# The second branch's projection as seven products of half blocks

## The chip, the cores and the metric

One core of one Trainium2 chip runs the program. The metric is the device time of one execution in microseconds. A core has TensorE (matmuls, results in PSUM banks), VectorE (DVE), ScalarE (ACT) and GpSimd (POOL), each with a queue of its own that is worked off in order, and SyncE (SP), which here only issues transfers. POOL issues transfers too, among them all that add to what lies at their destination.

## The reference, cut to what matters

One layer over 1024 prompt tokens and 32 sample tokens, 1056 columns in all; the model width is 1024.

```python
y_A = sink_attention(...)                 # (t, 1024)
y_B = rms_norm(hgrn2(...)) * silu(og_B)   # (t, 1024)
mix = sigmoid(gate_A) * (y_A @ W_brA) + sigmoid(gate_B) * (y_B @ W_brB)
x = x + rms_norm(mix @ W_out)
[a | u] = rms_norm(x) @ W_up;  a = conv3(a)
x = x + rms_norm((gelu(a) * u) @ W_down)
x = x + (pe @ W_ple) * sigmoid(x @ W_ple_gate)    # pe: (t, 256), the per-layer inputs
```

All inputs and outputs are float32.

## The kernel before

Every product of float32 matrices is made of three matmuls of rounded parts: a matrix is split into a rounded part (a cast on ScalarE, "hi") and a remainder (a subtraction on VectorE, "lo"), and hi x hi, hi x lo and lo x hi are added in PSUM. Activations lie with the features on the 128 partitions (8 tiles, k = 0 to 7) and tokens in the columns; the 1056 tokens are 4 groups of 264 (H), or 2 halves (p) of 2 groups (h).

The stages follow each other on TensorE: the head stage (input projections, attention, the recurrence with its heads 0 to 7; functions `group_out`, `tile_out` and the list `pieces`, beside which `small` and `at` put other work at counted places), branch A's projection, branch B's projection, the out projection, the per-layer input's product (`ple_product`), the up stage (22 units), the down stage, the gate. What is late in one stage moves all that follow.

Branch A's projection is made of seven products of half blocks instead of eight (`a_unit`, operands numbered i = 0 to 6): the weights are taken in 2 x 2 blocks of 512 x 512, the activations in 2 x 2 blocks (features halves a, token groups h), and sums of blocks stand for some of them. The sums lie in DRAM (`wa_d` of the weights, `sa_d` of the activations) and are made beside the head stage by accumulating POOL transfers (`block_sum`). `OPS` gives two phases: for each of 4 columns c first the products 0, 1, 2, then for each column 3, 4, 5, 6. One product for one column and both token halves is a step: 24 matmuls (k 4 x 3 parts x 2 halves). The steps are counted by `n_s`: 0 to 11 half steps, then to 33 whole ones. `beside(n)`, called at the end of a step, runs what `during(step, ...)` put there: loading an operand into a page of memory (`a_page`, `a_load`) and splitting it (`a_split`, `halves`). Pages are named places ("l0", "r6", ...), reused when the last reader is done. The weights of a step come through a ring of 8 buffers "wb": `a_raw` loads two at a time, `a_prepare` casts and subtracts.

After a step its results are read from PSUM: product 0 by ScalarE ("as"), the others by VectorE, which combines them ("R", "ac") and multiplies by the gate (1 + tanh, "ta"). Products 2 and 4 are written to `mx_d` in DRAM, products 5 and 6 stay in memory (`M_`).

Branch B's projection is plain: 8 columns x 4 groups, each 8 k x 3 matmuls (`block`, `product`), then gate, addition of branch A's part, and the split for the out projection (`Ra`, `Rb`) at lines 1758 and 1759 and `split`. Between the columns `p_cols` turns the per-layer inputs: 24 transposes of 88 columns, split, and written to `pc_d`, read again by `p_load`.

The out projection takes two halves p; for each p 8 columns c and the two groups. Beside its second half run the norm of the first (`pair_norm`: sums at line 1822, a chain of small VectorE instructions, rows at line 306), `x1_part` and `build_ops`, which make the up stage's operands. The up stage's first weights (`early_parts`, tiles "rw" and "pw") are split beside its first half. After it come the sums of the remaining norms, in a bank of the pool `tr` (two banks).

The order of the instructions within each engine is set by the framework's scheduler, which goes by its own model of durations and by the constraints `behind(...)` (not before the last instruction of an engine).

Of the kernel before, what the change touches and what calls it, by code (L numbers as in the profile page):

```python
# [59 lines left out]
def layer_kernel(  # L60
# [50 lines left out]
    ghh = cp.tile([P, 1], F32, name="ghh")  # L111
# [7 lines left out]
    mx_d = dp.tile([P, 2, 4, 2, H], F32, name="mx_d")  # L119
    wa_d = {o: dp.tile([P, 4, 512], F32, name=f"wa_d{o}") for o in (1, 3, 4, 6)}  # L120
    sa_d = {o: dp.tile([P, 4, 2, H], F32, name=f"sa_d{o}") for o in (1, 3, 4, 5)}
# [7 lines left out]
    pc_d = [dp.tile([P, 2, 2, H], F32, name=f"pc_d{g}") for g in range(4)]  # L129
# [36 lines left out]
    plan += [rows_cols(w_br_b, 0, c * P, P, KT) for c in range(8)]  # L166
# [150 lines left out]
    with right("ap") as ap:  # L317
# [287 lines left out]
        with tc.tile_pool(name="np", bufs=1, side="right", reuse_waits="tile") as np_:  # L605
# [85 lines left out]
            def derived():  # L691
# [8 lines left out]
                V.tensor_scalar(ghh[:], gvec[:, 48:49], 0.5, None, op0=ALU.mult)  # L700
# [386 lines left out]
    with right("bp") as bp:  # L1087
# [297 lines left out]
        def group_out(h, g):  # L1385
# [73 lines left out]
        sums = [lambda n=n, c=c: w_sum(n, c) for n in range(8) for c in range(2)]  # L1459
        for n, (dst, (o, src, acc)) in enumerate([(sa_d, y) for y in y_sums] + [(wa_d, a) for a in a_sums]):  # L1460
            sums.insert(2 * n, lambda d=dst[o][:], src=src, acc=acc: block_sum(d, src, acc))
        for n, f in enumerate(sums):
            at(26 + 11 * n // 2, f)
# [33 lines left out]
    A_ORDER = [(c, i) for ph in OPS for c in range(4) for i in ph]  # L1497
# [3 lines left out]
    at_h, at_l = ("r3", "r4", "l7", "l6"), ("l2", "l3", "l4", "l5")  # L1501
    at_y = (("r6", "r5"), ("r1", "r7"), ("r0", "r2"), ("l0", "l1"))

    def a_raw():

        k = len(raw_a)
        t = wp.tile([P, KT, P], F32, tag="wr", name=nm("wa"), bufs=2)
        raw_a.append(t)
        for a in range(2):
            c, i = A_ORDER[2 * k + a]  # L1510
            src = wa_d[i] if i in wa_d else av[:, i // 2 % 2 + i // 5, i // 5]
            dma(t[:, 4 * a:4 * a + 4], src[:, :, c * P:(c + 1) * P])

    def a_prepare(n):

        while len(ready_a) < min(n + 1, len(A_ORDER)):
# [5 lines left out]
            S.copy(t[:, 0], src)  # L1522
            V.tensor_tensor(t[:, 1], src, t[:, 0].bitcast(F32), op=ALU.subtract)
# [4 lines left out]
    def a_page(i, p):  # L1528
        opa[i, p] = page_at(at_a[i][p], [P, 2, 4, H], "oa")

    def a_load(i, p, queue=dma):
        t = opa[i, p]
        src = sa_d[i][:, :, p] if i in sa_d else ya_v[:, min(i, 1), i // 6][:, :, p]
        queue(t[:, 1].bitcast(F32), src)
# [5 lines left out]
    def a_split(i, p):  # L1540
        halves(opa[i, p][:, 0], opa[i, p][:, 1])
# [19 lines left out]
    mctx = ExitStack()  # L1561
    mxp = mctx.enter_context(right("mxp"))
    M_ = {o: mxp.tile([P, 4, 2, H], F32, name=f"mx{o}") for o in (5, 6)}
    with right("mp") as mp:
# [11 lines left out]
        Ra, Rb, Ya, Yb = [None] * 4, [None] * 4, [None] * 4, [None] * 4  # L1576
        R_ = page_at("l6", [P, 4, 2, H], "R").bitcast(F32)

        tps_a = [(0, (0,)), (1, (0,)), (0, (1,)), (1, (1,)), (2, (0, 1)), (3, (0, 1))]
        gates_a = [(c, 0, tps) for c, tps in tps_a]  # L1580
        gates_a += [(a, h, (0, 1)) for c in range(4) for a, h in ((c + 4, 1), (c + 4, 0), (c, 1))]
        ta_a = []

        def a_gate(col, h, tps):

            while len(ta_a) < 3 and gates_a:
                c_, h_, p_ = gates_a.pop(0)
                t = mp.tile([P, 2, H], F32, tag="ta", name=nm("ta"), bufs=4)
# [3 lines left out]
            if col is None:  # L1592
                return
# [1281 lines left out]
```

## Time and profile before

| what | value |
|---|---|
| median of 3 runs | 1952.49 us (1950.92 to 1953.19) |
| the profiled execution | 1950.0 us |
| its span | 1948.2 us |
| TensorE busy | 1927.2 us (99%) |
| VectorE, ScalarE, POOL busy | 1453.3, 1012.4, 307.3 us |
| branch A's stage | about 849.8 to 933.3 us of the span |
| branch B's stage | 933.3 to 1028.1 |
| out projection | 1028.1 to 1123.7 |

The granted TensorE clock is 0.999 over the run. The profiled execution is one run; the times of the changed kernel are to be held against the median.

### The profile page before, as it was taken

To read this page: it belongs to the slowest core of one execution; us is meant where nothing else is said; L and a number is where in the kernel's file an instruction comes from. 1 tells how busy PE (TensorE), PEld (TensorE's weight loads), DVE (VectorE), ACT (ScalarE), POOL (GpSimd) and SP (SyncE) were. 2 spreads that over 40 slices of the span, in tenths; PEclk is the share of its full clock that TensorE was granted. 3 is DMA by queue.
4 is the path that set the end of the run, shared out by engine and by line. 5 is a ranking of instruction groups with operands and counts; after the bars stand their busy time and mean duration, and the time that the engine had idled before them with its cause. 6 is when DMAs were issued, how large, how long until landed. Compare 5 with 4: busy or idle time off the path is not lost. (4 is left out here: it accounts for less than half of the span.)

```text
span 1948.2 us, 38057 instructions
## 1 busy us (share of the span) xinstructions
PE 1927.2 (99%) x14619; PEld 1910.0 (98%) x14619; DVE 1453.3 (75%) x3160; ACT 1012.4 (52%) x2182; POOL 307.3 (16%) x419
## 2 busy tenths in 40 slices
PE   8999999999999999999999999999999999999998
PEld 8999999999999999999999999999999999999998
DVE  6777777788888888657755778788787786768872
ACT  7667777666666666553324763333333336534432
POOL 2111111010101110100001123343543410000000
PEclk9999999999999999999999999999999999999999
DMA  8534543434637563487748582444565357654342
GB/s 269 156 108 122 139 121 97 139 104 103 155 113 166 96 120 75 124 292 226 219 148 289 182 290 92 140 131 152 131 147 148 104 179 235 220 185 153 115 132 87
DMA packets 310507, 302.19 MB, mean 155 GB/s; under 512 B 14293, under 2 KB 276344, under 8 KB 310325
## 3 DMA queue, kind: packets, MB, share of 16 engines
q1 hardware_dynamic: 277269, 229.57, 37.8%
q0 software_dynamic: 32928, 70.14, 15.8%
q8 instruction: 115, 1.88, 0.4%
q14 instruction: 67, 0.55, 0.1%
q10 hardware_dynamic: 128, 0.06, 0.0%
HBM read 213.48 MB, written 115.16 MB: 169 GB/s over the span
## 5 line engine op out<-in xcount | busy, mean ns | idle before, releaser
L2304 PE MATMUL st<-op,wt 128*128 128x264 f32 x1232 | 348.8, 283 | 2.1 <-ACT Sp L2315 1.4
L2306 PE MATMUL st<-op,wt 128*128 128x264 f32 x1232 | 349.7, 284 | 0.0
L2305 PE MATMUL st<-op,wt 128*128 128x264 f32 x1232 | 347.7, 282 | 0.0
L2304 PEld LDWEIGHTS st<-op,wt 128*128 128x128 f32 x1232 | 231.2, 188 | 3.5 <-ACT Sp L2315 2.0
L2305 PEld LDWEIGHTS st<-op,wt 128*128 128x128 f32 x1232 | 231.3, 188 | 0.0
L2306 PEld LDWEIGHTS st<-op,wt 128*128 128x128 f32 x1232 | 230.8, 187 | 0.0
L2428 PE MATMUL st<-dop,wt 128*128 128x264 f32 x616 | 174.4, 283 | 1.4 <-ACT S L2443 1.4
L2430 PE MATMUL st<-dop,wt 128*128 128x264 f32 x616 | 174.3, 283 | 0.0
L2429 PE MATMUL st<-dop,wt 128*128 128x264 f32 x616 | 173.9, 282 | 0.0
L1972 ACT CAST wt<-wu 128x512 fp32r<-128x512 f32 x126 | 76.0, 619 | 177.7 <-POOL wu L1981 70.9
L205 PE MATMUL mm<-La,wh 128*128 128x384 f32 (+1 forms) x480 | 158.2, 330 | 0.0
L206 PE MATMUL mm<-Lb,wh 128*128 128x384 f32 (+1 forms) x480 | 155.3, 324 | 0.6 <-DVE Lb L781 0.4
L207 PE MATMUL mm<-La,wl 128*128 128x384 f32 (+1 forms) x480 | 154.9, 323 | 0.1
L1973 DVE TENSOR_TENSOR wt<-wu,wt 128x512 fp32r<-128x512 f32 x126 | 86.4, 694 | 44.9 <-ACT wt L1972 44.9
L2428 PEld LDWEIGHTS st<-dop,wt 128*128 128x128 f32 x616 | 115.6, 188 | 1.9 <-ACT S L2443 1.6
L2429 PEld LDWEIGHTS st<-dop,wt 128*128 128x128 f32 x616 | 115.7, 188 | 0.0
L2430 PEld LDWEIGHTS st<-dop,wt 128*128 128x128 f32 x616 | 115.4, 188 | 0.0
L2078 ACT CAST wt<-wd 128x512 fp32r<-128x512 f32 (+1 forms) x84 | 49.1, 586 | 91.7 <-PE st L2430 71.9
L206 PEld LDWEIGHTS mm<-Lb,wh 128*128 128x128 f32 x480 | 90.4, 189 | 1.7 <-DVE Lb L781 1.4
L207 PEld LDWEIGHTS mm<-La,wl 128*128 128x128 f32 x480 | 90.2, 188 | 0.5 <-DVE wl L756 0.5
L1119 PE MATMUL G<-La,wt 128*128 128x288 f32 x288 | 90.4, 314 | 0.0
L205 PEld LDWEIGHTS mm<-La,wh 128*128 128x128 f32 x480 | 90.2, 188 | 0.2
(602 smaller groups left out, 6240.8 us busy)
## 6 DMA issues: line engine op xcount, KB each, us to landing
wu<-in_w_up_dram SPq DMA_DIRECT2D x42, 512.0 KB
wu<-in_w_in_dram SPq DMA_DIRECT2D x36, 512.0 KB
w_d<-in_w_down_dram POOLq DMA_DIRECT2D x24, 704.0 KB, 6.9
a_d<-Up SPq DMA_DIRECT2D x22, 528.0 KB
wr<-in_w_in_dram SPq DMA_DIRECT2D x21, 512.0 KB
s_d<-sm SPq DMA_DIRECT2D x40, 264.0 KB
dop<-s_d SPq DMA_DIRECT2D x16, 528.0 KB
wr<-in_w_out_dram SPq DMA_DIRECT2D x16, 512.0 KB
```

Of the source, the lines that this page charges most:

```text
L205: E.matmul(ps, wh, a, start=first and n == 0, stop=False)
L206: E.matmul(ps, wh, b, start=False, stop=False)
L207: E.matmul(ps, wl, a, start=False, stop=last and n == len(ks) - 1)
L1119: E.matmul(o, wh, x[0][k], start=first and k == 0, stop=False, skip_group_check=True)
L1972: S.copy(t[:, 0], src)
L1973: V.tensor_tensor(t[:, 1], src, t[:, 0].bitcast(F32), op=ALU.subtract)
L2304: E.matmul(o, wh, xh, start=first and k == 0, stop=False, skip_group_check=True)
L2305: E.matmul(o, wh, xl, start=False, stop=False, skip_group_check=True)
L2306: E.matmul(o, wl, xh, start=False, stop=k == 3, skip_group_check=True)
L2428: E.matmul(o, wh, xh_, start=first and k == 0, stop=False, skip_group_check=True)
L2429: E.matmul(o, wh, xl_, start=False, stop=False, skip_group_check=True)
L2430: E.matmul(o, wl, xh_, start=False, stop=k == ng - 1, skip_group_check=True)
```

## The change

Branch B's projection is built like branch A's: `a_unit` gets the branch as a parameter (br 0 or 1), with own sums of weights (`wb_d`) and operands (`sb_d`), own pages (`at_b`) and 28 more steps, 34 to 61 (34 to 45 the first phase, 46 to 61 the second). All four of branch A's results go to `mx_d`. In branch B the transfer that brings branch A's result adds it onto the gated product in memory (`accum_op`), and three steps later `out_parts` splits the sum for the out projection; in the last column of the second phase VectorE adds instead. One weight split takes a negative sign, and the sign of some parts of y_B is set in `group_out`, which now works on pieces of the groups and writes them to `sb_d` as well. The sums of w_down that stood in the head stage (two of four columns) move to the up stage, where POOL now issues two per unit instead of one. The transposes of the per-layer inputs move beside the second half of the out projection (one of 12 behind each block from column 2 on), and their parts stay in memory. For odd groups the out projection takes k = 3 last.

```diff
-    pc_d = [dp.tile([P, 2, 2, H], F32, name=f"pc_d{g}") for g in range(4)]
+    bv = w_br_b[0].rearrange("(k a p) (h n) -> p a h k n", a=2, p=P, h=2)
+    yb_v = yb_d.rearrange("p (k a) (t h c) -> p a h k t c", a=2, t=2, h=2)
...
-            V.scalar_tensor_tensor(sg[:, :n], t[:, :n], ghh[:, 0:1], sg[:, :n],
-                                   op0=ALU.mult, op1=ALU.mult)
+            for a, e in PIECES[g]:
+                q, z_ = a // H, slice(a - o, e - o)
+                neg = (h + q) % 2
+                V.scalar_tensor_tensor(sg[:, z_], t[:, z_], ghh[:, neg:neg + 1], sg[:, z_],
+                                       op0=ALU.mult, op1=ALU.mult)
             dma(yb_d[:, h, o:o + n], sg[:, :n])
+            for a, e in PIECES[g]:
+                q = a // H
+                first = ((4, 3), (5, 1))[h % 2][q % 2]
+                dma(sb_d[first][:, h // 2, q // 2, a % H:a % H + e - a], sg[:, a - o:e - o])
...
+        b_sums = [(3, bv[:, 0, 0], 0), (4, bv[:, 0, 1], 0), (1, bv[:, 0, 0], 0), (6, bv[:, 1, 0], 0),
+                  (3, bv[:, 0, 1], 1), (4, bv[:, 1, 1], 1), (1, wb_d[4][:], 1), (6, wb_d[1][:], 1)]
+        def yb_sum(n, k):
+            o, src = ((4, yb_v[:, 0, 1]), (3, yb_v[:, 1, 1]), (1, sb_d[4]), (5, sb_d[1]))[n]
+            block_sum(sb_d[o][:, k], src[:, k], 1)
...
+    at_b = {**at_a, 3: ("l0", "l1"), 4: ("l2", "l3"), 5: ("l4", "l5"), 6: ("r6", "r5")}
+        def out_parts(c, h, t, ps=(0, 1)):
+            for p in ps:
+                split(Ra[2 * p + h][c], Rb[2 * p + h][c], t[:, p])
...
+                    ta, (a, h) = ta_a.pop(0), C_AT[i]
+                    last = br == 1 and c == 3 and ph
+                    for z_ in (slice(0, 1), slice(1, 2)) if last and i == 6 else (sl,):
...
+                        V.scalar_tensor_tensor(g, g, 1.0, x, op0=ALU.add, op1=ALU.mult)
+                        if last:
+                            V.tensor_tensor(g, g, ma_a[i][:, z_], op=ALU.add)
+                            out_parts(c + 4 * a, h, ta, range(z_.start, z_.stop))
+                    if br == 0:
+                        gdma(mx_d[:, 2 * a + h, c, sl], ta[:, sl])
+                    elif not last:
+                        gdma(ta[:], mx_d[:, 2 * a + h, c], accum_op=ALU.add)
+                        during(n_s[0] + 3, both, out_parts, c + 4 * a, h, ta)
...
+        for p in range(2):
+            during(44 + p, a_page, 6, p, 1)
+            during(44 + p, a_load, 6, p, dma, 1)
+            during(47 + p, both, a_split, 6, p, 1)
...
+    KO = tuple((k, k) for k in (0, 1, 2, 4, 5, 6, 7, 3))
-        order = [(c, g) for g in range(4) for c in range(2)]
-        order += [(c, g) for c in range(2, 8) for g in range(4)]
...
+        if i == 0:
+            p_bank[:] = [tr_bank(), tr_bank()]
+        for k in range(2):
+            E.transpose(p_bank[k][:, 88 * i:88 * i + 88], p_raw[n][:88, k * P:(k + 1) * P], ident[:88, :88])
+        p_load()
...
-                z_out(c, g, block(w, ALL, Ra[g], Rb[g], KS, H))
+                z_out(c, g, block(w, ALL, Ra[g], Rb[g], KO if g % 2 else KS, H))
+                if p and c > 1:
+                    with behind(E):
+                        p_cols(2 * c + g - 6)
...
-                if 2 <= u < 18 and n == 4:
-                    w_sum((u - 2) // 2, 2 + u % 2)
+                if 2 <= u < 18 and n in (1, 4):
+                    w_sum((u - 2) // 2, 2 * (u % 2) + n // 4)
```

What the scheduler makes of it, at three places, the first of them on two engines. The numbers behind the names tell buffers apart. First ScalarE (fence 1) in branch B's second phase, from the weight of step 48 to that of step 51: "wt" is a weight's rounded part, "ta" a gated product, "Ra" its rounded part for the out projection; ta_12180 is that of step 45, ta_12282 that of step 47. Before, at the same place of branch A:

```order
L1522 CAST wt_11611<-wa_11541 128x512
L1537 CAST Ya_11467<-Yb_11468 128x1056
L1522 CAST wt_11645<-wa_11541 128x512
L1537 CAST Ya_11467<-Yb_11468 128x1056
L1522 CAST wt_11682<-wa_11608 128x512
```

Now, in branch B:

```order
L228 CAST wt_12617<-wa_12538 128x512
L228 CAST Ra_12147<-ta_12180 128x264
L228 CAST Ra_12149<-ta_12180 128x264
L228 CAST wt_12652<-wa_12538 128x512
L228 CAST wt_12688<-wa_12614 128x512
L228 CAST Ra_12534<-ta_12282 128x264
L228 CAST Ra_12536<-ta_12282 128x264
L228 CAST wt_12724<-wa_12614 128x512
```

Before, only casts of loaded operands stood between the weights; now casts of a product that a transfer has added to do.

Second VectorE (fence 2) in steps 47 to 49: "ac" reads a product from PSUM (st), "wt" is a weight's remainder, "ta" the gate product, "ob" an operand's remainder; ob_12459 and ob_12497 are the two halves of the operand of product 6. Before, in branch A's second phase:

```order
L1641 TENSOR_TENSOR ac_11606<-ac_11606,st_11578 128x528
L1523 TENSOR_TENSOR wt_11718<-wa_11608,wt_11718 128x512
L1642 SCALAR_TENSOR_TENSOR ta_11503<-ta_11503,ac_11606 128x528
L1538 TENSOR_TENSOR Yb_11468<-Yb_11468,Ya_11467 128x1056
L1646 TENSOR_TENSOR ac_11672<-R_11004,st_11577 128x528
```

Now:

```order
L1662 TENSOR_TENSOR ac_12532<-ac_12532,st_12504 128x528
L229 TENSOR_TENSOR wt_12652<-wa_12538,wt_12652 128x512
L1664 SCALAR_TENSOR_TENSOR ta_12282<-ta_12282,ac_12532 128x528
L1558 TENSOR_TENSOR ob_12459<-ob_12459 128x1056
L1662 TENSOR_TENSOR ac_12602<-Rb__12080,st_12503 128x528
L229 TENSOR_TENSOR wt_12688<-wa_12614,wt_12688 128x512
L1664 SCALAR_TENSOR_TENSOR ta_12387<-ta_12387,ac_12602 128x528
L1558 TENSOR_TENSOR ob_12497<-ob_12497 128x1056
L1662 TENSOR_TENSOR ac_12644<-st_12504,Rb__12080 128x528
```

The remainder at this place was of an operand of the next stage; now it is of the operand of step 49, and its second half stands behind the read of step 48.

Third ScalarE (fence 3) where the out projection begins: "pw" are parts of the up weights, ta_12901 is the last column's product 5, whose cast the first out block needs:

```order
L184 CAST wh_13114<-wr_13112 128x1024
L1995 CAST pw_13174<-rw_13172 128x512
L1995 CAST pw_13175<-rw_13172 128x512
L228 CAST Ra_12147<-ta_12901 128x264
L228 CAST Ra_12149<-ta_12901 128x264
```

Before, the last such cast stood ahead of the up weights:

```order
L228 CAST Ra_11973<-tb_13084 128x264
L184 CAST wh_13241<-wr_13239 128x1024
L228 CAST Ra_11974<-tb_13115 128x264
L1972 CAST pw_13227<-rw_13225 128x512
L1972 CAST pw_13228<-rw_13225 128x512
```

The two have changed places. Last VectorE (fence 4) in the second half of the out projection, "pc" being the remainders of the turned inputs, read from the two banks of the pool tr:

```order
L1850 TENSOR_TENSOR x_2209_13851<-x_2209_13851,z_13098 128x1056
L1913 TENSOR_TENSOR z_13097<-z_13097,z_13098 128x1056
L229 TENSOR_TENSOR pc_13985<-tr_13902,pc_13985 128x264
L229 TENSOR_TENSOR pc_13985<-tr_13903,pc_13985 128x264
L1802 TENSOR_TENSOR sqz_13107<-sqz_13107,sq_14016 128x264
```

Before:

```order
L1850 TENSOR_TENSOR x_2235_13900<-x_2235_13900,z_13151 128x1056
L1913 TENSOR_TENSOR z_13150<-z_13150,z_13151 128x1056
L1802 TENSOR_TENSOR sqz_13160<-sqz_13160,sq_14046 128x264
```

Two remainders come in, behind an addition and a subtraction of 1056 columns. On TensorE the third pair of transposes (the last into these banks) is followed by 48 matmuls and then the first pair of the next group.

## Rows read from the trace of the kernel before

**Rows 1.** The page: span and busy time of each engine.
```profile
span 1948.2 us, 38057 instructions
PE 1927.2 (99%) x14619; PEld 1910.0 (98%) x14619; DVE 1453.3 (75%) x3160; ACT 1012.4 (52%) x2182; POOL 307.3 (16%) x419
```

**Rows 2.** TensorE's waits: line, waited for: us, times, longest.
```profile
PE tr L744 <- POOL ident masks.py:199: 2.6, 1, 2.6
PE st L1620 <- ACT as L1629: 1.6, 2, 1.4
```

**Rows 3.** Windows: length, busy (count) per engine, clock, DMA share, GB/s.
```profile
640.00:700.00 60.00, 60.00 (x405) 59.76 (x404) 51.69 (x146) 37.79 (x100) 6.63 (x10) 1.00 0.54 107
...
855.27:933.30 78.03, 77.83 (x640) 1.00 0.84 256
...
933.30:1028.10 94.80, 94.80 (x795) 1.00 0.57 171
```

**Rows 4.** VectorE's groups, 850 to 1130: busy, mean ns, idle before.
```profile
L1523 DVE TENSOR_TENSOR wt<-wa,wt 128x512 fp32r<-128x512 f32 x24 | 16.5, 688 | 7.5 <-ACT wt L1522 7.4
...
L1538 DVE TENSOR_TENSOR oa<-oa 128x1056 fp32r<-128x1056 f32 x11 | 13.8, 1253 | 3.9 <-ACT oa L1537 3.8
...
L229 DVE TENSOR_TENSOR pc<-tr,pc 128x264 fp32r<-128x264 f32 x8 | 3.1, 423 | 0.0
...
L1642 DVE SCALAR_TENSOR_TENSOR ta<-ta,ac 128x528 f32<-128x528 f32 x4 | 2.8, 704 | 0.1
```

**Rows 5.** ScalarE's groups in the same stretch.
```profile
L1522 ACT CAST wt<-wa 128x512 fp32r<-128x512 f32 x23 | 14.3, 621 | 28.5 <-PE st L1624 13.2 <-DMA wa<-wa_d 7.4 <-DMA wa<-in_w_br_a_dram 5.2
L228 ACT CAST Ra<-tb 128x264 fp32r<-128x264 f32 x32 | 13.2, 413 | 52.6 <-DVE tb L1759 50.1 <-DVE nv L1830 2.5
...
L228 ACT CAST pc<-tr 128x264 fp32r<-128x264 f32 x8 | 3.0, 377 | 0.0
```

**Rows 6.** VectorE's timeline, branch A's second phase: start, us [idle before].
```profile
893.33 0.69 DVE L1523 TENSOR_TENSOR wt<-wa,wt 128x512 fp32r<-128x512 f32 x1 [2.62 <-ACT wt L1522]
893.94 0.70 DVE L1641 TENSOR_TENSOR ac<-ac,st 128x528 f32<-128x528 f32 x1
894.55 0.69 DVE L1523 TENSOR_TENSOR wt<-wa,wt 128x512 fp32r<-128x512 f32 x1
```

**Rows 7.** The tile mx_d: landing of its POOL transfers.
```profile
DMA to landing us min/median/max: 2.4/5.4/6.8
```

**Rows 8.** The tile wr: landing of accumulating POOL transfers of 512 KB.
```profile
DMA to landing us min/median/max: 4.5/4.7/7.2
```

**Rows 9.** The tile w_d: landing of the sums of 704 KB.
```profile
DMA to landing us min/median/max: 6.1/7.3/19.3
```

**Rows 10.** SP's timeline: the up weights' load.
```profile
1025.85 1.05 SPq L2002 DMA_DIRECT2D rw<-in_w_up_dram  x2
```

**Rows 11.** ScalarE's timeline: their first cast.
```profile
1031.23 1.14 ACT L1972 CAST pw<-rw 128x512 fp32r<-128x512 f32 x2 [1.49 <-DMA rw<-in_w_up_dram]
```

**Rows 12.** TensorE's timeline: the norm's rows in the out projection.
```profile
1085.00 1.54 PE L306 MATMUL tr<-ident,nr 88*128 88x88 f32 x12 [0.21 <-DVE nv L2123]
```

**Rows 13.** VectorE's timeline in the out projection.
```profile
1102.66 1.26 DVE L1850 TENSOR_TENSOR x<-x,z 128x1056 f32<-128x1056 f32 x1 [1.03 <-DMA x<-xt_d]
1103.84 1.25 DVE L1913 TENSOR_TENSOR z<-z,z 128x1056 f32<-128x1056 f32 x1
```

**Rows 14.** ScalarE's timeline at the out projection's end.
```profile
1123.95 0.48 ACT L1796 ACTIVATE z<-mm,gph 128x264 f32<-128x264 f32 x1 [2.13 <-PE mm L207]
1124.33 0.38 ACT L1801 ACTIVATE sq<-mm 128x264 f32<-128x264 f32 x1
```

**Rows 15.** VectorE's timeline there.
```profile
1124.75 0.43 DVE L1802 TENSOR_TENSOR sqz<-sqz,sq 128x264 f32<-128x264 f32 x1 [1.84 <-ACT sq L1801]
```

**Rows 16.** POOL's groups in the up stage, 1200 to 1720.
```profile
L1986 POOL TENSOR_TENSOR wu<-wu 128x512 f32<-128x512 f32 x19 | 28.6, 1505 | 70.5 <-DVE wt L1973 70.5
...
L1449 POOL DMA_DIRECT2D w_d<-in_w_down_dram x12 | 16.1, 1338 | 0.0
```

More of the change, by code (lines that the diff above doesn't have):

```diff
@@ L1496, in layer_kernel @@
     OPS = ((0, 1, 2), (3, 4, 5, 6))
-    A_ORDER = [(c, i) for ph in OPS for c in range(4) for i in ph]
+    A_ORDER = [(b, c, i) for b in range(2) for ph in OPS for c in range(4) for i in ph]
     raw_a, ready_a, n_a = [], [], [0]
@@ L1521, in a_prepare, with a_page, a_load @@
             t = wp.tile([P, 2, 4, P], F32R, tag="wb", name=nm("wt"), bufs=8)
-            S.copy(t[:, 0], src)
-            V.tensor_tensor(t[:, 1], src, t[:, 0].bitcast(F32), op=ALU.subtract)
+            if A_ORDER[k][::2] == (1, 2):
+                split(t[:, 0], t[:, 1], src, -1.0)
+            else:
+                split(t[:, 0], t[:, 1], src)
             ready_a.append(t)
     opa = {}
[L1528 to L1534, printed above, removed]
+    def a_page(i, p, b=0):
+        opa[b, i, p] = page_at(BR[b][4][i][p], [P, 2, 4, H], "o" + "ab"[b])
+    def a_load(i, p, queue=dma, b=0):
+        _, _, sums, y, _ = BR[b]
+        src = sums[i][:, :, p] if i in sums else y[:, min(i, 1), i // 6][:, :, p]
+        queue(opa[b, i, p][:, 1].bitcast(F32), src)
     def halves(hi, lo):
@@ L1651, in a_unit, with ma_load @@
             return kept
-        a_gate(None, 0, ())
+        ma_a = {}
+        def ma_load(i):
+            a, h = C_AT[i]
+            ma_a[i] = mp.tile([P, 2, H], F32, tag="as", name=nm("ma"), bufs=2)
+            dma(ma_a[i][:], mx_d[:, 2 * a + h, 3])
+        gate_loads()
         steps_a = {}
@@ L1693, in beside @@
             n_s[0] += 1
-        ws = [a_unit(0, c, (0,), beside=beside) for c in range(2)]
+        ws = [a_unit(0, 0, c, (0,), beside=beside) for c in range(2)]
         for c in range(2):
-            a_unit(0, c, (1,), ws[c], beside)
+            a_unit(0, 0, c, (1,), ws[c], beside)
         for c in range(2, 4):
-            a_unit(0, c, beside=beside)
+            a_unit(0, 0, c, beside=beside)
         for c in range(4):
-            a_unit(1, c, beside=beside)
-        assert not steps_a
-        Ra = [columns8(s, "Ra") for s in at_h]
-        Rb = [columns8(s, "Rb") for s in at_l]
+            a_unit(0, 1, c, beside=beside)
+        R_.append(mp.tile([P, 4, 2, H], F32, name="Rb_"))
+        for ph in range(2):
+            for c in range(4):
+                a_unit(1, ph, c, beside=beside)
+        assert not steps_a, steps_a
         qctx.close()
@@ L1929, in layer_kernel, with p_load, p_cols @@
     ple_w, pT = [], {}
-    def p_load(g):
-        pool, tag = (oz, "pc") if g < 2 else (wp, "wr")
-        xs = pool.tile([P, 2, 2, H], F32R, tag=tag, name=nm("pc"), bufs=2)
-        dma(xs[:].bitcast(F32), pc_d[g][:])
-        pT[g] = xs
+    p_raw, p_bank = [], []
+    def p_load():
+        n = len(p_raw)
+        if n == 12:
+            return
+        r = oz.tile([P, 256], F32, tag="pr", name=nm("pr"), bufs=2)
+        t0 = 88 * n
+        m_ = min(88, 1024 - t0)
+        dma(r[:m_], p_prompt[0, 0, t0:t0 + m_, :])
+        if m_ < 88:
+            dma(r[m_:88], p_sample[0, 0])
+        p_raw.append(r)
+    def p_cols(n):
+        g, i = divmod(n, 3)
+        if i == 0:
[3 more added lines that the diff above has]
+        p_load()
+        if i == 2:
+            pool, tag = (oz, "pc") if g < 2 else (wp, "wr")
+            xs = pT[g] = pool.tile([P, 2, 2, H], F32R, tag=tag, name=nm("pc"), bufs=2)
+            for k in range(2):
+                split(xs[:, 0, k, :], xs[:, 1, k, :], p_bank[k][:, :H])
     def ple_product(g, beside):
```

180 lines of the change are left out of this document (67 added, 113 removed).

## The prediction

> **What bounds the kernel now.** I read the engine line of the page first: TensorE is busy 1927 of 1948 us, VectorE three quarters, ScalarE half [rows 1]. Then TensorE's waits: the longest of the whole run is 2.6 us, before its first matmul, and the next line has 1.6 in two [rows 2]. So nearly every TensorE instruction taken out shortens the run, and nearly every new wait of TensorE lengthens it; the other engines matter only where TensorE waits for them. Third the windows, for the pitch of a product: in branch a's stage 640 matmuls of 264 columns took 78.03 us, 121.9 ns each (the mean duration of 283 ns is pipelined and is not the pitch); in the head stage TensorE is busy 60.00 of 60 us beside a VectorE at 51.7 [rows 3].
>
> **What goes.** The second branch's projection is now 8 columns x 4 groups x 8 k x 3 = 768 matmuls; seven products of half blocks, over 4 columns x 2 token halves x 4 k x 3, are 672. 96 x 121.9 ns = 11.7 us. The 24 transposes of the per-layer inputs move, they do not go: (94.80 - 768 x 0.1219) / 24 = 50 ns each in the old stage, 1.2 us in either place. What is left to work out is what the new stage makes TensorE wait for, at four places.
>
> **Place 1, the seventh product of column 0 (step 49).** Its operand reuses the pages of product 0, so it is split late: half 0 in step 47, half 1 in step 48, used in step 49. VectorE's queue has, after the products of step 47 end: read, a weight remainder, gate product, remainder of the half; and the same after step 48 (order fence 2). These are 0.70, 0.69, 0.70 and 1.25 us [rows 4], issued 0.61 us apart [rows 6]: 0.2 + 3 x 0.61 + 1.25 = 3.3 us after a step's end, while a step is 24 x 0.122 = 2.93. Half 0 alone would be 0.2 late. Half 1 is needed 13 matmuls (1.6 us) into step 49 and comes 3.1 us after half 0: 3.1 - 1.5 = 1.6 us more. Reasons of the order alone give 1.9 us.
>
> To this comes the cast of that weight. ScalarE has two casts of the transferred sum of step 45 ahead of it (order fence 1). The sum: step 45 ends 5.85 us before step 47 does; 0.8 for read and gate, 0.54 to issue, then the landing. The nearest row is the same tile going out by the same queue: 5.4 us, 2.4 to 6.8 [rows 7]; accumulating transfers of twice the size landed in 4.7, 4.5 to 7.2 [rows 8]. With 5.4: -5.85 + 0.8 + 0.54 + 5.4 = 0.9; two casts of 0.41 and one of 0.62 [rows 5] bring 2.3, then 0.69 + 0.61 + 1.25 = 4.9 against a need at 3.05. Half 0 is then 1.9 late instead of 0.2. I take 3.5 us in all. Ends: 1.9 (landing hides), 8 (landing 6.8, which also holds up two further casts). Below 1.9 only if the queue order did not hold.
>
> That a weight's cast can hold up the reads behind it is in the trace already: at 893.33 VectorE had idled 2.6 us for a weight before it read the next product [rows 6].
>
> The Trainium skill ("DMA: Bandwidth & Descriptors", section on the anatomy of a DMA on the SWDGE path) fits such a transfer as 2.0 us plus bytes over 436 GB/s, so by it 264 KB would be there in an estimated 2.6 us; place 1 would then cost 1.9 and the result would be 1.6 us lower. The trace does not agree for the loaded stage: 5.4 at the median, and only its shortest, 2.4, is near the rule.
>
> **Place 2, from branch b into the out projection.** The first out block needs the last column of product 5 as its last k. On ScalarE its cast now stands behind two casts of the up weights (order fence 3), whose page is freed by product 5's first half. Loading them took from 1025.85 to 1031.23, 5.4 us [rows 10, 11]. From the end of step 60: -1.46 + 0.3 + 5.4 = 4.2, two casts 1.2, the wanted cast 0.41, its remainder 0.43: 6.3. Out starts at 2.93 and gets to its eighth k 21 matmuls later, 5.5 to 5.6: 0.7 late; the next block's last k (a chain of read, gate, sum and split after step 61) 0.3 more. I take 1.0. Ends: 0 (weights land a microsecond sooner) and 3.3 (2.5 us later).
>
> **Place 3, transposes in the out projection.** Both transpose banks hold one group of three; the next group's first transpose waits until VectorE has taken the remainders of the last, and it stands 48 matmuls after it. In the old trace the sums of the row norms run at 1085.00 to 1086.54 [rows 12]; 141 matmuls and 6 transposes after it is 1104.1. VectorE at that place waits for a load until 1102.66, adds, subtracts until 1105.1 [rows 13], and only then come the two remainders (order fence 4): banks free at 1105.45 and 1105.8. 1.4 + 0.35 = 1.75 us. The two later groups follow 33 and 28 matmuls behind, with VectorE busy without a gap there; I count nothing for them since the first wait has put TensorE behind. Ends: 0 and 4.
>
> **Place 4, the norm after it.** Its bank is that of the last group. The last read begins at 1123.95 and its square ends at 1124.7 [rows 14]; a cast (0.38) follows it, VectorE's sum starts at 1124.75 [rows 15], then the remainder (0.42, rows 4): free at 1125.5. TensorE has two transposes and seven products (0.95 us) to do and is there at 1124.7. 0.8 us; ends 0 and 2.
>
> **What costs nothing, and what hides it.** The head stage: 16 sums of down weights leave the POOL queue there, 8 of branch weights and 12 of operands come; 24 gate products are cut in two (24 x about 0.15 us of VectorE), beside a TensorE without a gap [rows 3]. More issues stand on SP and POOL there, at a DMA share of about a half [rows 3]. If that cover went it would be up to the 3.6 us of VectorE. The up stage: 16 issues more on POOL, 1.3 us each, ahead of its last addition of a unit; that addition waits 70 us over 19 units for VectorE, 3.7 each [rows 16], so 1.3 fits. Without that gap: 16 x 1.3 = 21 us at most. The weights of branch b are smaller loads of the kind that branch a lives on (there ScalarE idles 13 us for TensorE to free a place of the ring, so it is ahead; rows 5).
>
> **Sum.** -11.7 + 3.5 + 1.0 + 1.75 + 0.8 = -4.65 us. The profiled execution took 1950.0, which gives 1945.35; the median of the runs shown, 1952.49, is 2.5 above it, so the median after is 1947.8. Its own range, with the ends of the four places taken one at a time, is 1945 to 1952.
>
> **Rivals.**
> A, the waits are hidden: landings at their shortest (2.4 and 4.5) leave place 1 at 1.9 and places 2 to 4, whose ends reach down to 0, at 0.4 together. -11.7 + 2.3 = -9.4: 1943.1. For it: waits of TensorE over 2 us hardly exist now [rows 2]. Against: the four chains above are of queue order, not of load.
> B, the handovers eat the gain: place 3 at 4, its two later groups 1 each, place 1 at 5 and places 2 and 4 as above give 12.8 - 11.7 = +1: 1953.6, no change. For it: VectorE waits for a load right there [rows 13]; against: TensorE once late waits less.
> C, slower: the accumulating transfers land late. Each of the 13 sums is waited for by ScalarE, whose next cast is a weight that stands in front of VectorE's read of the next product, whose gate product is the next sum: a loop. A landing later than 5.4 is paid at five handovers (the third product of the last column, steps 48 and 49, the first accumulation of the next two columns), so about 5 us per us. At 7.3, the median of the sums in memory [rows 9]: 5 x 1.9 = 9.5, 1957.3. It is slower than before by 0.2% from a landing of 7.1 on (8.6 / 5 = 1.7). For it: the longest of rows 8 is 7.2, and branch b also writes and reads the sums of branch a. Against: the median of the nearest row is 5.4.
> D, the change does not take the matmuls out or the pitch rises: then no 11.7, and 1952 or more; the instruction list has exactly 96 fewer TensorE rows, so hardly.
>
> **How the numbers follow.** Forecast 0.50, A 0.17, B 0.16, C 0.15, D 0.02. 0.2% of 1952.5 is 3.9 us, about what a measurement of this kernel can tell from no change. Faster by more is below 1948.6: all of A and some 0.56 of the forecast, 0.28: 0.45. Slower by more is above 1956.4: C and a little of D: 0.16. The rest, 0.39, within. The range is 1942 to 1958: it leaves out the half of C that lands later than 7.3 and the lowest corner of A.
>
> **What would show it.** Right: TensorE's count lower by 96; in the stage of branch b a wait of TensorE for a split operand (line of the halves' remainder) of 1.5 to 2 us twice in the first column of four products, and no other over 1 us; one of about 0.7 for the out projection's operand; one of 1 to 2 for a transpose bank in the out projection's second half. Wrong: b's stage at 82 us without such waits (A), or repeated waits in columns 2 and 3 with ScalarE idle for the transferred sums (C); a changed up stage or head stage would mean that a cover I counted on was not there.

## The result: slower by 0.4%, and the profile after

Six executions of the changed kernel took 1956.43 to 1961.01 us, median 1960.32; six of the kernel before 1950.55 to 1953.19, median 1951.20. Ratio 1.0042, interval 1.0029 to 1.0055: slower. Forecast was 1947.8 with 1942 to 1958; the median lies outside.

The profiled execution is the shortest of the six, 1956.43. Its span and engine line, for [rows 1]:

```profile
span 1954.7 us, 38121 instructions
PE 1921.2 (98%) x14523; PEld 1901.4 (97%) x14523; DVE 1466.1 (75%) x3189; ACT 1027.3 (53%) x2212; POOL 343.9 (18%) x464
```

TensorE has the 96 instructions less, and is busy 6.0 us less; the span is 6.5 us longer, so it stands still 12.5 us more. Its waits, for [rows 2] (line, waited for: us, times, longest):

```profile
PE tr L1952 <- DVE pc L229: 2.5, 1, 2.5
PE mm L205 <- ACT Ra L228: 2.5, 1, 2.5
PE st L1640 <- DVE ac L1662: 2.3, 2, 1.5
...
PE st L1642 <- DVE ob L1558: 1.5, 1, 1.5
PE st L1640 <- ACT as L1649: 1.4, 1, 1.4
```

Windows of branch A's stage, of branch B's, and of 3.4 us in the out projection, for [rows 3] (length, then busy time and count of PE, PEld, DVE, ACT and POOL, the granted clock, the DMA share, GB/s):

```profile
851.10:938.40 87.30, 82.59 (x672) 81.75 (x673) 61.59 (x87) 37.35 (x55) 13.11 (x21) 1.00 1.00 299
938.40:1022.40 84.00, 81.98 (x675) 81.58 (x673) 59.09 (x94) 34.03 (x62) 11.98 (x15) 1.00 0.90 232
...
1105.60:1109.00 3.40, 3.40 (x19) 3.40 (x17) 3.40 (x4) 1.37 (x4) 0.00 (x0) 0.51 0.18 57
```

Branch B takes 84.0 us instead of 94.8: the gain is there. Branch A, whose products did not change, takes 87.3 instead of 83.5, with the DMA engines at 1.00 instead of 0.84. And in the out projection the granted clock falls to its lower level, which it did nowhere in this stretch before.

By TensorE's first instruction of each stage, in us:

| stretch | before | after | change |
|---|---|---|---|
| head, up to branch A | 849.8 | 851.2 | +1.4 |
| branches A and B, up to the first out block | 178.3 | 173.9 | -4.4 |
| out projection, up to the norm sums | 95.6 | 104.3 | +8.7 |
| the rest of the span | 824.5 | 825.3 | +0.8 |

The two branches nearly without waits would give -13.6 (below, noyb3). Of the 9.2 us between, 9.1 are seven waits that the timeline of TensorE shows: 4.6 in branch A, 2.0 in branch B, 2.5 before the first out block. In the out projection 3.2 are waits, about 1.6 the low clock and 2.0 the transposes. Another 0.9 is order only: seven products of the per-layer inputs now stand ahead of the norm sums, where before they stood behind them, so the last row of the table is less by as much. Before, then now:

```profile
1123.76 1.03 PE L1822 MATMUL tr<-ones,sq 128*88 128x1 f32 x12
...
1125.11 0.37 PE L205 MATMUL st<-pc,wq 128*128 128x264 f32 x1
```

```profile
1127.66 0.37 PE L205 MATMUL st<-pc,wq 128*128 128x264 f32 x1
...
1129.38 1.10 PE L1822 MATMUL tr<-ones,sq 128*88 128x1 f32 x12 [0.62 <-DVE pc L229]
```

The last 1.0 of the 8.7 I cannot assign.

### The profile page after: what moved, and what is told of

It reads as the page before. It is cut to its first block, busy times and chain, and to the rows that moved or that the text cites. A ratio compares the mean times of both kernels' runs of the same rounds, so it can differ in the third digit from the quotient of the medians.

```text
span 1954.7 us, 38121 instructions
## 1 busy us (share of the span) xinstructions
PE 1921.2 (98%) x14523; PEld 1901.4 (97%) x14523; DVE 1466.1 (75%) x3189; ACT 1027.3 (53%) x2212; POOL 343.9 (18%) x464
## 4 chain that ended last, share of the span: by engine, by line
PE 39%; issue 5%; DVE 3%; DMA 2%; ACT 1%; POOL 0%; ACTq 0%; POOLq 0%; DVEq 0%; SPq 0%
PE st L2330 7%; PE st L2329 7%; PE st L2328 7%; PE st L2452 4%; PE st L2454 4%; PE st L2453 4%; PE st L205 2%; PE st L206 2%; PE st L207 2%; DMA pw_d<-pw 1%; DMA ta<-mx_d 1%; DVE wt L1996 0%; PE mm L205 0%; PE mm L206 0%; PE mm L207 0%
## 5 line engine op out<-in xcount | busy, mean ns | idle before, releaser
L2453 PE MATMUL st<-dop,wt 128*128 128x264 f32 x616 | 173.9, 282 | 0.0
```

The costliest lines, as they stand in the source:

```text
L2453: E.matmul(o, wh, xl_, start=False, stop=False, skip_group_check=True)
```

## The experiments

All are the changed kernel or edits of it. Time: median (executions), and ratio to the kernel before run beside it (medians 1949.6 to 1950.3), 95% interval.

| run | edit | time | ratio |
|---|---|---|---|
| after_again | none | 1960.14 (5) | 1.0049, 1.0037 to 1.0062 |
| trbank | first out blocks in other banks | 1954.26 (11) | 1.0021, 1.0012 to 1.0030 |
| pmm | more banks for the transposes | 1952.67 (11) | 1.0012, 1.0003 to 1.0020 |
| noyb3 | four sums left out | 1952.19 (11) | 1.0012, 1.0003 to 1.0020 |
| ybmove | four sums elsewhere | 1953.83 (12) | 1.0019, 1.0010 to 1.0029 |
| yb3plain | four copies for four sums | 1956.14 (10) | 1.0027, 1.0018 to 1.0036 |
| last19 | the last sum four steps later | 1959.80 (5) | 1.0047, 1.0033 to 1.0061 |
| early6 | split for place 1 a step earlier | 1963.76 (6) | 1.0071, 1.0058 to 1.0084 |
| allfix | trbank, pmm, ybmove, early6 | 1951.31 (11) | 1.0002, 0.9993 to 1.0011 |
| fix3 | trbank, pmm, ybmove | 1943.76 (5) | 0.9968, 0.9956 to 0.9981 |
| late4 | casts of sums a step later | 1958.10 (5) | 1.0042, 1.0028 to 1.0056 |
| fix3_late4 | fix3 and late4 | 1946.65 (8) | 0.9980, 0.9970 to 0.9990 |

**after_again.** 

> The changed kernel once more, unaltered, for a profile of an ordinary execution: the profiled one took 1956.4 us, the other five 1959.7 to 1961.0. Theory 1 (clock): about 1960.3 us again, and in the profile a second stretch of granted clock 0.50, some 3.4 us long, that the first profile does not have (it has one, at 1105.6 to 1109.1, after the transposes' bank wait of 2.53 us); the likeliest place is behind the 2.5 us wait at the start of the out projection. Theory 2 (transfers): no second stretch at 0.50; instead the weights of branch A's stage land later still, and that stage takes 90 us or more instead of 87.3.

Span 1956.6. Two stretches at the low clock, though not behind the out projection's first wait: one after a 2.68 us wait at 911.87, and a longer one behind the norm sums. The row of the norm sums' wait (timeline: start, us, engine, line, op, out<-in, idle before) and a window in each stretch:

```profile
1128.79 1.10 PE L1822 MATMUL tr<-ones,sq 128*88 128x1 f32 x12 [0.63 <-DVE pc L229]
```

```profile
912.00:914.00 2.00, 2.00 (x10) 2.00 (x11) 2.00 (x3) 0.00 (x0) 0.49 (x1) 0.50 1.14 316
1130.40:1136.90 6.50, 6.50 (x32) 6.50 (x33) 2.13 (x14) 1.20 (x2) 0.76 (x1) 0.50 0.35 141
```

The stretch of low clock behind the transposes, which the first profile has, is missing here: from one execution to the next it falls at different places. The way from branch A's first product to the first out block took 175.2 us, 1.3 more than in the first profile. So part of what separates the ordinary execution from the first profile is the clock.

**trbank.**

```diff
-    def block(w, wsl, xh, xl, ks, n):
-        b = mm_bank()
+    def block(w, wsl, xh, xl, ks, n, b=None):
+        b = b or mm_bank()
-  z_out(c, g, block(w, ALL, Ra[g], Rb[g], KO if g % 2 else KS, H))
+  z_out(c, g, block(w, ALL, Ra[g], Rb[g], KO if g % 2 else KS, H, None if p or c else tr_bank()))
```

> The first two blocks of the out projection write into the two banks for transposes, so that they do not wait for the banks of branch B's last products. Theory 1 (bank handover): TensorE's 2.5 us wait at the start of the out projection is for the last read of product 6 by VectorE, since the new pool of banks lies on the old one; with other banks it starts at once and waits at most 0.4 us at its eighth k. 2.1 us faster than the changed kernel, 4 us if a clock drop behind that wait goes too: 1956 to 1958. Theory 2 (operand): the wait is for ScalarE's cast of the last column of product 5, as the profile's wait line names it; then it stays at 2.2 us or more, only somewhat later in the block, and the time stays at 1960.

The two rows of the changed kernel in question, from the timelines of TensorE and VectorE:

```profile
1025.12 0.36 PE L205 MATMUL mm<-Ra,wh 128*128 128x264 f32 x1 [2.52 <-ACT Ra L228]
```

```profile
1024.56 0.42 DVE L1662 TENSOR_TENSOR ac<-st,Rb__12080 128x264 f32<-128x264 f32 x1
```

TensorE waits ahead of its first out matmul, which reads k = 0, and goes on as VectorE has read the second half of product 6 out of its bank (1024.98). The profile names the cast that happened to end then. With the transpose banks:

```profile
1010.00:1030.00 20.00, 20.00 (x165) 19.80 (x164) 16.70 (x33) 8.98 (x19) 2.20 (x3) 1.00 0.87 229
```

No gap. The bank it was; the eighth k does not wait at all. The time fell by 5.9 us and not by the 2 to 4 expected; the wait itself is 2.5 of them, and what the rest is I cannot tell from one profile.

**pmm.**

```diff
-            p_bank[:] = [tr_bank(), tr_bank()]
+            p_bank[:] = [(mm_bank if g % 2 else tr_bank)() for _ in range(2)]
```

> The second and fourth group of the turned per-layer inputs take two banks of the out projection's six instead of the two transpose banks, so that no group waits for the remainders of the one before. Theory 1: the 2.5 us wait goes, and with it the 3.4 us at half clock behind it (1.6 us lost) and the 0.6 us of the norm sums: 4 us or more faster than the changed kernel, about 1956, with granted clock 1.00 in the whole second half of the out projection. Theory 2 (the wait moves): the third group or the norm waits instead, granted clock falls there, and the gain is under 1 us: 1959 or more.

In the changed kernel, VectorE and then TensorE at the third group of pairs:

```profile
1101.15 1.26 DVE L1850 TENSOR_TENSOR x<-x,z 128x1056 f32<-128x1056 f32 x1 [0.60 <-DMA x<-xt_d]
1102.32 1.25 DVE L1913 TENSOR_TENSOR z<-z,z 128x1056 f32<-128x1056 f32 x1
1103.49 0.77 DVE L229 TENSOR_TENSOR pc<-tr,pc 128x264 fp32r<-128x264 f32 x2
```

```profile
1103.97 0.37 PE L1952 MATMUL tr<-ident,pr 88*128 88x88 f32 x2 [2.53 <-DVE pc L229]
...
1106.04 0.42 PE L205 MATMUL mm<-Ra,wh 128*128 128x264 f32 x1
1106.26 0.42 PE L206 MATMUL mm<-Rb,wh 128*128 128x264 f32 x1
```

This is the chain of place 3, and behind it the matmuls start 0.22 us apart instead of 0.122. With pmm the whole stretch from the first out block to the norm sums is busy at full clock, and so is the norm:

```profile
1024.20:1122.50 98.30, 98.17 (x817) 98.00 (x818) 69.57 (x112) 60.57 (x122) 13.50 (x21) 1.00 0.71 231
```

98.3 us instead of 104.3, 0.9 of the difference because the seven products stand behind the norm sums again. Theory 1, and below its number: 1952.67 where about 1956 was expected, 7.5 us under the changed kernel. The profiled execution is one of the shorter, 1949.8.

**noyb3.**

```diff
-        for n in range(4):
-            during(12 + n, yb_sum, n, 3)
```

> Leaves out the four accumulating transfers of y_B's last quarter (264 KB each) that run beside branch A's stage, so the sums for branch B lack that part; all else as in the changed kernel. Theory 1 (these sums fill the DMA engines): branch A's stage falls from 87.3 to about 84 us, its DMA share from 1.00 to 0.92, and the time by 3 us. Theory 2 (the rest of the added traffic does: writes of products 5 and 6, branch B's operands): the stage stays at 86 us or more and the time within 1.5 us of the changed kernel's.

Both stages in one window, 1344 matmuls:

```profile
850.36:1015.10 164.74, 164.24 (x1344) 163.18 (x1344) 121.32 (x181) 71.38 (x116) 20.73 (x31) 1.00 0.94 267
```

122.6 ns a matmul, 13.6 us less than the two stages before, with nearly no wait, and a median 8.0 us lower where 3 were expected. But the reason given was not right: between 849 and 938 us the DMA share is 0.99, against 0.98 in after_again, and 311 GB/s were moved against 298. The engines are as full without the sums; so I read it that the sums take away not total traffic but the weights' place in it. In the changed kernel POOL issued two sums at 872.72, and the weights that SP had issued at 872.34 were cast at 882.26, ScalarE having idled 6.44 us; here the same weights, issued at 871.44, were there at 878.53:

```profile
882.26 0.62 ACT L228 CAST wt<-wa 128x512 fp32r<-128x512 f32 x1 [6.44 <-DMA wa<-in_w_br_a_dram]
```

```profile
878.53 0.62 ACT L228 CAST wt<-wa 128x512 fp32r<-128x512 f32 x1 [3.13 <-DMA wa<-in_w_br_a_dram]
```

Behind the late cast stood ScalarE's reading of product 0, for which TensorE waited 1.45 us at 886.02. In total ScalarE idled for weights nearly as long without the sums as with them; what differs is the longest single wait. ScalarE in branch A's stage, before, changed and here (us in total, times, longest):

```profile
ACT wt L1522 <- DMA wa<-wa_d: 7.4, 5, 5.0
```

```profile
ACT wt L228 <- DMA wa<-wa_d: 13.8, 5, 6.8
```

```profile
ACT wt L228 <- DMA wa<-wa_d: 13.2, 6, 4.8
```

**ybmove.**

```diff
+        at(len(pieces) - 6, yb_sum, 0, 3)
...
+    small.setdefault(5, []).append(lambda: yb_sum(2, 3))
     stream(tail[3:], small)
...
-        for n in range(4):
-            during(12 + n, yb_sum, n, 3)
+        during(27, yb_sum, 1, 3)
+        during(30, yb_sum, 3, 3)
```

> The same four sums of y_B's last quarter, all made, but not four in a row at steps 12 to 15: the first beside the head's last gates, the one that operand 1 needs at the end of the head stage, the two that are needed late at steps 27 and 30. Theory 1 (they hold up the weights of branch A's stage where they stand): the three waits at about 885, 898 and 912 us go, branch A's stage takes about 84 us instead of 87 to 88, and the time is that of the kernel without these sums, 1952 to 1953, against 1960 for the changed kernel. Theory 2 (the sum of the traffic counts, whenever it runs): the waits come at other steps, and the gain is under 2 us: 1958 or more.

Theory 1, with all sums made, at 1953.83 a little above its number. The DMA engines are as full as before, and TensorE does not wait, though two of the four sums still run beside branch A's stage (issued at 921.82 and 927.57):

```profile
870.00:980.00 110.00, 110.00 (x911) 110.00 (x910) 78.13 (x110) 48.52 (x73) 13.73 (x21) 1.00 1.00 295
```

Ahead of this window one wait is longer than in the changed kernel, 1.93 us at 860.51 against 0.87.

**yb3plain.**

```diff
-            block_sum(sb_d[o][:, k], src[:, k], 1)
+            block_sum(sb_d[o][:, k], src[:, k], k < 3)
```

> The four transfers stay at steps 12 to 15 but copy instead of adding, so branch B's operands are not the sums. Theory 1 (any transfer there takes the engines from the weights): the waits of branch A's stage stay, 1959 to 1961. Theory 2 (adding is what is dear: a transfer that adds holds the DMA engines longer than one that copies): the transfers land in 3 to 4 us instead of 7.4, the waits shrink by half or more, 1955 or less.

Landing of these transfers, in the changed kernel and here:

```profile
DMA to landing us min/median/max: 6.8/7.4/8.3
```

```profile
DMA to landing us min/median/max: 4.7/5.6/5.8
```

Between the theories: the waits at about 885 and 912 go, the one at 898 grows from 0.84 to 2.08 us, and the time falls by 4.0 us, half as much as without the sums. Adding took some 2 us more of landing per transfer; the copy costs too.

**last19.**

```diff
-            during(12 + n, yb_sum, n, 3)
+            during((12, 13, 14, 19)[n], yb_sum, n, 3)
```

> Of the four sums only the last one moves, from step 15 to step 19, so that POOL does not stand for 7 us on the landing of the third (in the first profile until 893.98) with the write of a gated product behind it (ready at 891.8, issued at 894.51). Theory 1 (queues: that write frees the place for a gate's load, which stood 5.9 us on SP at 896.16 with the weights behind it): the wait at about 912 (1.5 to 2.7 us, in every profile that has the sums at steps 12 to 15) goes or falls under 0.5 us, the one at about 885 (0.8 to 1.6) stays, since the weights of that step were already out beside the first two sums; 2 to 4 us faster than the changed kernel, 1956 to 1958. Theory 2 (the engines' load alone): the same bytes in the same 20 us, so the waits at 885 and at 912 both stay, 1959 to 1961.

My theory of queues falls, and theory 2 is right in the time alone. The write was no longer held up, the wait at 885 went down to 0.67 and the one at 898 to 0.20, but the one at 912 grew. The sum now stood at 899.22 on POOL; SP's weights beside it (timelines of SP, ScalarE, TensorE):

```profile
899.23 4.93 SPq L1530 DMA_DIRECT2D wa<-wa_d  x2
```

```profile
910.66 0.62 ACT L228 CAST wt<-wa 128x512 fp32r<-128x512 f32 x1 [8.74 <-DMA wa<-wa_d]
```

```profile
912.76 0.56 PE L1640 MATMUL st<-oa,wt 128*128 128x264 f32 x1 [3.60 <-ACT wt L228]
```

The delay went where the sum went: the first of the two weights was cast 11.4 us after its issue. In after_again, where POOL had no sum under way at that step, it was 8.1 us, from an issue at 901.64:

```profile
909.76 0.62 ACT L228 CAST wt<-wa 128x512 fp32r<-128x512 f32 x1 [6.61 <-DMA wa<-wa_d]
```

The Trainium skill ("DMA: Bandwidth & Descriptors", section on SWDGE vs HWDGE vs iDMA) says that each DMA engine serves the queues of the two paths in turn; by that a sum of POOL's takes turns from SP's weights that are under way. The 11.4 us against 8.1 fit this; no run here shows the turns themselves.

**early6.**

```diff
-            during(47 + p, both, a_split, 6, p, 1)
+            during(46 + p, both, a_split, 6, p, 1)
```

> The operand of product 6 of branch B is split one step earlier (steps 46 and 47 instead of 47 and 48). Place 1 of the prediction by itself: the wait of TensorE in step 49 for the second half's remainder (1.5 us in the first profile, 1.6 in the second) goes, everything else stays: 1958.5 where it goes alone, up to 3 us less if a stretch at half clock goes with it. Rival (the operand's load has not landed a step earlier, so ScalarE's cast of it holds up the weights behind it): a wait of 1 us or more in steps 47 to 49, 1960 or more.

Worse, as the rival had it, but not for its reason. ScalarE waited only 0.38 us for the operand's load, and the wait in step 49 shrank to 0.92 us, with a new one of 1.12 us ahead of it. The scheduler, with the splits a step earlier, put the casts of a transferred sum ahead of a weight's cast further on, in the third column: TensorE waited 4.50 us at 1009.65. **allfix** holds the same edit. 

> The changed kernel with all four edits: the sums moved, the first two out blocks in the transpose banks, every second group of turned inputs in banks of the out projection, the operand of product 6 split a step earlier. Theory 1 (the gain of 11.7 us is there and was given back at these places, with the stretches at half clock that follow the waits): no wait of TensorE over 1 us between 852 and 1150 us, granted clock 1.00 there, 1941 to 1944, that is about 6 us faster than the kernel before. Theory 2 (the gain is lost to a slower stage anyway, waits only move): 1948 or more.

It came out at theory 2's number, 1951.31, with two waits in branch B, 2.10 and 4.17 us. ScalarE, VectorE and TensorE at the second:

```profile
1002.29 0.72 ACT L228 CAST Ra<-ta 128x264 fp32r<-128x264 f32 x2 [6.64 <-DMA ta<-mx_d]
1002.92 0.61 ACT L228 CAST wt<-wa 128x512 fp32r<-128x512 f32 x1
```

```profile
1003.57 0.69 DVE L229 TENSOR_TENSOR wt<-wa,wt 128x512 fp32r<-128x512 f32 x1 [3.27 <-ACT wt L228]
...
1004.80 0.70 DVE L1656 TENSOR_TENSOR ac<-Rb__12080,st 128x528 f32<-128x528 f32 x1
```

```profile
1005.64 0.56 PE L1642 MATMUL st<-ob,wt 128*128 128x264 f32 x1 [4.17 <-DVE ac L1656]
```

A cast waits for an accumulating transfer, the weight's cast behind it, its remainder on VectorE, the read of a product behind that: a turn of rival C's loop, set off by an order of casts and not by later landings (median of the thirteen sums 5.0 us here, 4.8 in the changed kernel).

**fix3** leaves that edit away. 

> The changed kernel with three edits: the four sums moved, the first two out blocks in the transpose banks, every second group of turned inputs in banks of the out projection; the split of product 6's operand stays where the change put it. Theory 1 (the gain is there, given back at these three places with the half-clock stretches behind them): the version with the earlier split took 1951.3, and its profile loses 2.10 + 4.17 us in two waits of branch B and some 9.5 us at half clock, worth about 4.7, that this order of ScalarE's casts does not have; against it stands the 0.7 us wait in step 49. 1951.3 - 6.3 - 4.7 + 0.7 = 1941.0; 1940 to 1943, 0.4% faster than the kernel before. Theory 2 (the accumulating transfers' landing makes branch B's stage wait whatever the order): a wait of 2 us or more in branch B's second phase here too, 1946 or more.

Its engine line, and windows from branch A to the norm sums (the out projection starts at 1017.28):

```profile
span 1942.8 us, 38121 instructions
PE 1919.3 (99%) x14523; PEld 1900.2 (98%) x14523; DVE 1465.7 (75%) x3189; ACT 1025.7 (53%) x2212; POOL 345.1 (18%) x464
```

```profile
850.90:1018.30 167.40, 164.75 (x1353) 164.15 (x1354) 122.50 (x183) 71.08 (x116) 23.10 (x33) 1.00 0.96 273
1018.30:1117.00 98.70, 97.95 (x813) 97.19 (x812) 71.46 (x117) 62.76 (x128) 13.82 (x22) 1.00 0.73 237
```

Faster than both kernels: 0.32% under the one before (0.19 to 0.44%). Theory 1, 2.8 us above its number and 0.8 above its range; in branch B waits of 1.0 and 0.5 us are left, in branch A one of 1.1. The three edits alone brought 5.9, 7.5 and 6.3 us against 1960.14, 19.7 together; all in one 16.4.

**late4.**

```diff
-                        during(n_s[0] + 3, both, out_parts, c + 4 * a, h, ta)
+                        during(n_s[0] + 4, both, out_parts, c + 4 * a, h, ta)
```

> The changed kernel, with the cast of a transferred sum put four steps after its product instead of three, nothing else. Theory 1 (ScalarE's queue: a cast that waits for its transfer holds up the weight behind it, that weight the remainder behind it on VectorE): with 2.9 us more for the landing (median 5.3, longest 7.2 us) ScalarE idles less for these transfers (31 us in ten waits in the first profile), and the wait in step 49 falls from 1.5 to 0.5 us or less; 1 to 2 us faster, 1958 to 1959, the other waits as before. Theory 2 (queue order of VectorE alone, as the prediction had it for the larger part of place 1): the wait in step 49 stays at 1.4 us or more.

The wait in step 49 did fall:

```profile
983.72 0.39 PE L1642 MATMUL st<-ob,wt 128*128 128x264 f32 x1 [0.22 <-DVE ob L1558]
```

The time's interval overlaps that of after_again, so the 2 us are not shown. Nor was it the edit that shortened this wait. ScalarE casts the sum of step 45 (the one in question) behind the same weight as in the changed kernel, and in both the moment it lands; only the casts of the first two sums and of the last ones moved. It landed in 4.2 us instead of 4.6. The changed kernel, then late4:

```profile
980.30 0.73 ACT L228 CAST Ra<-ta 128x264 fp32r<-128x264 f32 x2 [2.66 <-DMA ta<-mx_d]
```

```profile
979.90 0.73 ACT L228 CAST Ra<-ta 128x264 fp32r<-128x264 f32 x2 [1.91 <-DMA ta<-mx_d]
```

**fix3_late4.** 

> The three edits together with the casts one step later. If both theories 1 hold, no wait over 0.5 us between the first phase of branch A and the end of the out projection: 1939.5 to 1941.5. If the later casts crowd at the start of the out projection (the last sums are cast at its first blocks), a wait of 1 us or more there, and 1941 or more, no better than without.

The second case: no better than fix3, the late casts cost a wait 9.5 us into the out projection, and the wait in step 49 stayed, with ScalarE's order of casts there as in fix3.

```profile
978.98 0.39 PE L1644 MATMUL st<-ob,wt 128*128 128x264 f32 x1 [1.43 <-DVE ob L1559]
...
1026.76 0.39 PE L205 MATMUL tr<-Ra,wh 128*128 128x264 f32 x1 [1.19 <-ACT Ra L228]
```

## Why the prediction was wrong, step by step

**The gain, -11.7: right.** 96 matmuls fewer, and the two stages take 13.6 us less where they hardly wait: 11.7, 1.2 of transposes that moved, and 0.7 net of old waits.

**What costs nothing: this is the step that failed.** I priced what stands in the head and in the up stage. In the up stage it held: POOL's wait for VectorE gave up 19.6 us, against 1.3 x 16 = 21 worked out from [rows 16]:

```profile
L2009 POOL TENSOR_TENSOR wu<-wu 128x512 f32<-128x512 f32 x19 | 28.2, 1483 | 50.9 <-DVE wt L1996 50.9
```

The head ended 0.5 to 2.7 us later in twelve of the thirteen profiles of this kernel and its edits, 0.4 sooner in one; with one profile of before that is not settled. The step failed at branch A's stage. The change makes 16 sums of operands and not only the 12 that I counted in the head: the four of the last quarter (`yb_sum` with k = 3) are called at steps 12 to 15 of branch A. They stand nowhere in my sum, and that stage got no term at all, though [rows 3] had its DMA share at 0.84 and [rows 5] had ScalarE idling 12.6 us there for weights. I wrote that ScalarE is ahead; it was not, it was just in time. Leaving these sums out brings 8.0 us of the median, moving them 6.3.

**Place 1, 3.5: too large, right in kind.** One wait came and not two: 1.5 and 1.6 us in the two profiles of the changed kernel, 0.7 to 1.0 in most others with this split, 0.1 to 0.2 in noyb3, yb3plain and late4. It is that of the first half (in the first profile its remainder is done at 984.06 and TensorE goes on at 984.11), for which I had 1.9; ahead of early6 I put it down to the second. The 1.6 us that I added for the second half did not come: TensorE had other matmuls to do between the halves, for VectorE got the product of step 49 only at 988.79, 4.7 us after TensorE had gone on without standing still. Queue order alone gives the 0.2 that I had for the first half. The rest is the landing of the sum that ScalarE casts first: in all twelve profiles with a wait here ScalarE casts that sum the moment it lands, and TensorE goes on 3.8 us after that cast. The sum landed in 4.1 to 4.2 us where the wait was 0.1 to 0.2, in 4.4 to 4.8 where it was 0.7 to 1.6; I had taken 5.4.

**Place 2, 1.0: wrong mechanism.** I let TensorE start the out projection at once and wait at its eighth k. It waited 2.5 us before the first matmul, for a bank: the new pool of six banks lies on the old one and its first tile waits for the last read of the old. The operand's cast, for which I had worked the chain out, cost nothing.

**Place 3, 1.75: right place and chain, too small.** 2.5 and 2.6 us in the two profiles. Counted from the first out block, TensorE came to these transposes after 76.3 us where I had 76.0, VectorE freed the bank after 78.8 where I had 77.4: its load and its chain of small instructions ran 1.4 us later, and I had taken them over from the old trace unmoved. The transposes also cost 0.16 us a pair and not 0.1: with pmm two pairs stand 3.09 us apart,

```profile
1091.29 0.32 PE L1952 MATMUL tr<-ident,pr 88*128 88x88 f32 x2
1094.38 0.32 PE L1952 MATMUL tr<-ident,pr 88*128 88x88 f32 x2
```

where 24 matmuls take 2.93; 2.0 us for twelve and not 1.2.

**Place 4, 0.8: right**, 0.62.

**No term at all: the clock.** In the profile of the kernel before it is 1.00 up to the last 3 us. Around the new waits it often fell to the lower of its two levels, and behind place 4's wait of 0.6 too, where TensorE then has 24 matmuls of one column in a row. Where that happened, place 3 was worth about 4 us and place 4 up to 4.

**The rivals.** B (the handovers eat the gain) is the nearest in mechanism: 1953.6 against 1960.3, with waits at the right places 2 to 4 and without branch A and the clock. C came nearest in time with 1957.3, for the wrong reason: the thirteen transfers that add landed sooner than the 5.4 us taken from [rows 7], not later, and the loop made TensorE wait long only in early6 and allfix. In the first profile:

```profile
DMA to landing us min/median/max: 4.1/4.8/7.2
```

A (waits hidden) is what the two branches do once the four sums are out. D falls with the windows.

What stays open: 1.0 us of the out projection in the first profile, by what way the four sums delay the weights, and why fix3 gains less than its three edits one by one.

## What to carry to other kernels

List every stage that gets an instruction, and ask of each whether its weights come just in time: idle time of a casting engine that ends with a load need not be slack, and a transfer put beside such a stage can be paid there, not where it belongs. It depends on the place in the stage: here four sums in four steps cost 6 to 8 us, two of them later in the same stage no wait. When one pool of PSUM banks follows another, its first tile may wait for the last read of the old one; give the first blocks banks that have long been free. A new wait of TensorE has to be priced with what the clock does behind it.

## What the runs showed of the hardware

In the thirteen profiles of the changed kernel and its edits the granted clock fell to 0.50 (1.2 instead of 2.4 GHz) in 24 stretches between 820 and 1180 us. TensorE had 28 waits of 2 us or more there. Around 15 of them it fell, and around all four of 3.6 us or more; the 2.5 us wait at the out projection's start was followed by it in 2 of 9 profiles, the one of the transposes, 2.5 to 3.7 us, in 5 of 9. Seven more stretches stand behind the norm sums, in 7 of the 9 profiles with a wait of 0.6 us there and then 24 matmuls of one column. Behind the same 24 matmuls without a wait it fell in 1 of 4, and once behind the norm's rows with a wait of 1.1 us. A stretch lasts 3.4 or 6.8 us. Matmuls stand 0.22 us apart in it against 0.122, so it costs up to 0.45 of its length. The Trainium skill ("TensorE: Matmul & The Clock Gate", section Terms) prices it as the throttled time by the share of pulses that are lost, which is 0.5 here; the 0.45 is a little less.

The same four transfers land in 7.4 us where they add and in 5.6 where they copy (medians of changed kernel and yb3plain).
